# Where the bank exchange and the retention's small steps stand in the order of a two-layer decoder kernel

## The chip, the cores and the metric

The kernel runs on one core of a Trainium2 chip. Five engines work side by side and each takes its own instructions in order: TensorE (PE, matrix products), VectorE (DVE), ScalarE (ACT), GpSimd (POOL) and SyncE (SP, which issues nearly all loads). Semaphores join them. The metric is the device time of one execution in microseconds (us). A change under about 0.2% cannot be told from none here.

## The reference

Two layers over 512 tokens of width 2048, all in float32. Each layer modulates a normalised x by vectors that come from c (`shift`, `scale`, `gate`), mixes, and adds. Layer 0 mixes by retention over 8 heads, layer 1 by latent attention:

```python
for i in range(DEPTH):
    mod = (c_act @ ada_w[i] + ada_b[i])[:, None, :]
    shift, scale, gate = jnp.split(mod, 3, axis=-1)
    h = rmsnorm(x, norm_g[i]) * (1.0 + scale) + shift
    ...
    x = x + gate * y

def retention_branch(h, pos, w_in, gn_g, w_out):
    proj = h @ w_in
    q, k, v, g = jnp.split(proj, ...)
    q = rope(q, pos); k = rope(k, pos) * (RET_DK ** -0.5)
    y = chunkwise_retention(q, k, v)
    mu = jnp.mean(y, axis=-1, keepdims=True)
    var = jnp.mean(jnp.square(y - mu), axis=-1, keepdims=True)
    y = (y - mu) * lax.rsqrt(var + EPS)
    y = y.reshape(B, S, RET_WIDTH) * gn_g
    return (jax.nn.silu(g) * y) @ w_out
```

## The kernel before

**Products.** A float32 operand is split into a high part (a cast by ACT, L135 and L330) and a low part (a subtraction by DVE, L136 and L332), and a product is three matmuls: high by high, high by low, low by high. A matmul of 128x128 by 128x512 follows the one before it after 0.227 us.

**The opening** (L407 to L717) starts the projection of layer 0 while the modulation is still being summed. The 16 tiles of the 2048 columns of h ("kt") go in 8 units of two. For each unit PE does three groups of 24 matmuls, 5.44 us each: `products` of `here` and of g for both kt, and `bank_products` of `there`; `here` and `there` are v and qk by turns. v and qk need four PSUM banks each and share four, so `swap` (L385) changes them over: for each bank ACT copies its sums out (L390) and the other kind's sums in (L394), 8 copies, about 5 us. For the next unit `sum_mod` multiplies and sums two modulation loads for each kt on DVE (L356, 2.2 us each, 4 in a unit), `make_first` forms h and its high part on ACT (L370 to L381) and the low part hT on DVE (L382), and the weights of the next unit are split. `prepare_ahead(u, first, between)` and `prepare_behind` write this out; `queued` and `behind` (L422 to L433) tie what they issue behind the last instruction on ACT, DVE, PE and SP, so the code's order there is the engines' order. Unit 1 alone passes its products and its swap as `first` into `prepare_ahead`. In the last unit the tables of the rotation are made on DVE, and then the sums of h (L450 to L455), ahead of the first weights of the step list.

**The step list** follows. A step has the load and split of one tile of weights (`prepare`), its matmuls (`multiply`) and lists of small pieces `beside` it. The loop near L2180 issues, for step i: the loads, the split of the weights of step i+1 (`prepare_for`), the pieces `form` (on ACT and DVE), the matmuls, the pieces `multiply`, and then the modulation sums that have landed. A scheduler places the PE rows that `behind` does not tie, by its own estimate of when their inputs are ready.

**The retention** of a head (L1146 to L1296) is 14 pieces, one for each step, beside the out-projection of the heads ahead of it (L1390, names `o`, weights `o_r`, `o_whi`, `o_wlo`; 24 matmuls, 5.44 us in a step): rotations of q and k (`rope`, `qk_0p`), `scores` (s), their decay, `split_v` (v's parts), `values` (y), `group_norm` (statistics L1233 and L1234, the factor -mean/sd `nmr` L1239, and `yn` L1245, which reads y's banks), `gate`, `transposes` (yT), and `form_input`: the out-projection's operands `o_h` (ACT, L1275) and `o_l` (DVE, L1276). There are three rounds of 16 such steps with two heads each (heads 2 to 7), ahead of them heads 0 and 1. The even head's last pieces fall in the middle of a round; the odd head's `form_input` falls into the step that opens the next round, whose second step reads it. `light` says which steps of a round also load a row of the modulation of later stages (`mod`, L1092, a DVE sum of 1.2 us each).

Of the kernel before, what the change touches and what calls it, by code (L numbers as in the profile page):

```python
# [18 lines left out]
NT = T // P  # L19
# [30 lines left out]
def hybrid_trunk_kernel(  # L50
# [62 lines left out]
    def small(name, n=1):  # L113
        return base.tile([P, n], F32, tag="small", bufs=24, name=name)
# [316 lines left out]
    def queued(fn, *args):  # L431
        with behind(A_, V_, T_, S_):
            return fn(*args)  # L433
# [227 lines left out]
    for u in range(1, NU):  # L661

        here, there = ("v", "qk") if u % 2 == 0 else ("qk", "v")
        more = u + 1 < NU
        turns0 = [(kind, kt) for kind in (here, "g") for kt in (2 * u, 2 * u + 1)]
        if u == 1:
            def go_on_first():
                for turn in turns0:
                    queued(products, *turn)
                queued(swap, here, there)  # L670

            load_unit(2)
            prepare_ahead(2, low, go_on_first)
        elif more:
            load_unit(u + 1)
            prepare_ahead(u + 1, low)
        else:
            for i in range(7):
                if i == 2:
                    queued(low)  # L680
                queued(next, tables)
        if u == NU - 2:
            next(tables)
        if u > 1:
            for turn in turns0:
                queued(products, *turn)
        if more:
            if u > 1:
                queued(swap, here, there)
            low = prepare_behind(u + 1)  # L690
        else:
            for b, ps in enumerate(banks["qk"]):
                st = tmp(f"qk0_st{b}")
                queued(ACT.copy, st, ps)
                POOL.dma_start(qk_d[b * P : (b + 1) * P, :], st)
            queued(swap, None, "v")
            for _ in tables:
                pass
            for n, t in enumerate(ret_tables):
                POOL.dma_start(tables_d[n * P : (n + 1) * P, :], t)  # L700
            sum_parts = [queued(form_sums, n, hT, sums1, staged0, None, True) for n in range(2)]
            for b, ps in enumerate(banks["g"]):
                st = tmp(f"g0_st{b}")
                queued(ACT.activation, st, ps, AF.Silu)
                POOL.dma_start(g_d[b * P : (b + 1) * P, :], st)
        queued(bank_products, there, u)
# [24 lines left out]
    class Step:  # L731
# [3 lines left out]
        def __init__(self, load=None, prepare=None, multiply=None, follow=None, rows=0, sums=None):  # L735
            self.units = [(load, prepare)] if load else []
            self.multiply, self.follow = multiply, follow or (lambda: None)
            self.rows, self.sums = rows, sums
            self.beside = {"load": [], "form": [], "multiply": []}

    def plain_steps(nu, kn, parts, cn, name, take, n, lhs, rhs, evac, seeded=False, **kw):

# [418 lines left out]
    def retention(h, own, own2=None):  # L1161
# [64 lines left out]
                    mm3(ps, (s_hl[m][0][:, o : o + P], s_hl[m][1][:, o : o + P]), act_row(v[m]), m == 0, m == i)  # L1226
                ys.append(ps)

        def group_norm():
            stats = small(f"bn_{h}", 2 * NT)  # L1230
            for i in range(NT):
                st = l1_tile("st6", 4, f"st_{h}_{i}", (P, 6))
                DVE.bn_stats(out=st, in_=ys[i])  # L1233
                DVE.bn_aggr(out=stats[:, 2 * i : 2 * i + 2], in_=st)  # L1234
            var = small(f"var_{h}", NT)
            DVE.tensor_copy(var, stats.rearrange("p (i s) -> p i s", s=2)[:, :, 1])
            r = rsqrt(var, NT, 1.0, f"gn_{h}")
            nmr = small(f"nmr_{h}", NT)
            DVE.scalar_tensor_tensor(  # L1239
                out=nmr, in0=stats.rearrange("p (i s) -> p i s", s=2)[:, :, 0], scalar=-1.0, in1=r,  # L1240
                op0=ALU.mult, op1=ALU.mult,
            )
            for i in range(NT):
                y = l1_tile("yn", 4, f"yn_{h}_{i}")
                ACT.activation(y, ys[i], AF.Identity, bias=nmr[:, i : i + 1], scale=r[:, i : i + 1])  # L1245
                yn.append(y)
# [14 lines left out]
        def form_input():  # L1261
# [25 lines left out]
            {"load": load_decay, "multiply": scores},  # L1287
            {},
            {"load": load_v, "form": decay_scores},
            {"load": load_gates, "form": split_v, "multiply": values},  # L1290
            {"form": group_norm},
            {"form": gate},
            {"multiply": transposes},
            {"form": form_input},
        ]

    def place(pieces, block, first):
# [134 lines left out]
    for n in range(3):  # L1432
        block = []
        cols = range(4) if n % 2 == 0 else range(3, -1, -1)
        for r, after in zip(cols, [*cols[1:], None]):
            block += round_steps(n, r, go_on(n, r, after))
        heads += [retention(2 * n + 2 + i, big) for i in range(2)]
        light(block, (0, 2, 3, 4, 6, 7, 10, 11, 12, 14, 15, 0, 3, 7, 11, 15))
        steps += block


# [718 lines left out]
    for i, step in enumerate(steps):  # L2160
# [8 lines left out]
        with behind(S_):  # L2169
# [7 lines left out]
                    nc.sync.dma_start(tables[n], tables_d[(n0 + n) * P : (n0 + n + 1) * P, :])  # L2177
            for load in step.beside["load"]:
                load()
        n_prepared += prepare_for(i + 1)  # L2180
        with behind(V_, A_):
            for form_ in step.beside["form"]:
                form_()
        with behind(T_):
            step.multiply()
# [290 lines left out]
```

## Time and profile before

| | |
|---|---|
| median of 3 runs | 2158.71 us (2158.55 to 2159.61) |
| the profiled execution | 2156.47 us, its span 2154.7 us, granted clock 0.999 |
| opening, unit 1 to unit 7 | 51.83 to 163.4 us |
| step list: heads 0 and 1 and what leads to them | to about 1030 us |
| the three rounds | about 1030 to 1370 us |
| layer 1 | the rest |

In the profile's rows a start time comes first, then the duration, the engine, the line of the kernel, the operation, what it writes and reads without buffer numbers, and in brackets how long the engine had been idle before it and whose end ended that. A matmul's duration of 0.39 overlaps the next one. A window's row has the busy time of each engine, then the granted clock of PE, the share of the DMA engines and GB/s.

### The profile page before, as it was taken

To read this page: it belongs to the slowest core of one execution; us is meant where nothing else is said; L and a number is where in the kernel's file an instruction comes from. 1 tells how busy PE (TensorE), PEld (TensorE's weight loads), DVE (VectorE), ACT (ScalarE), POOL (GpSimd) and SP (SyncE) were. 2 spreads that over 40 slices of the span, in tenths; PEclk is the share of its full clock that TensorE was granted. 3 is DMA by queue.
4 is the path that set the end of the run, shared out by engine and by line. 5 is a ranking of instruction groups with operands and counts; after the bars stand their busy time and mean duration, and the time that the engine had idled before them with its cause. 6 is when DMAs were issued, how large, how long until landed. Compare 5 with 4: busy or idle time off the path is not lost.

```text
span 2154.7 us, 30027 instructions
## 1 busy us (share of the span) xinstructions
PE 2130.0 (99%) x11100; PEld 1825.1 (85%) x11100; DVE 1675.9 (78%) x2481; ACT 1056.5 (49%) x1604; POOL 106.8 (5%) x178
## 2 busy tenths in 40 slices
PE   8999999999999999999999999999999999999998
PEld 5788898988889888888888888898889989888887
DVE  7998788888878789766777787667978788886745
ACT  5674444445444444434344445345446565664434
POOL 1010000000000000000000000010001000000000
PEclk9999999999999999999999999999999999999999
DMA  9975686877777768765746566553456544346733
GB/s 382 404 277 193 220 275 225 277 236 259 257 257 256 230 234 281 247 204 167 241 159 232 188 219 244 167 174 112 165 181 208 181 135 147 116 135 222 242 108 137
DMA packets 229782, 462.96 MB, mean 215 GB/s; under 512 B 20817, under 2 KB 84337, under 8 KB 225793
## 3 DMA queue, kind: packets, MB, share of 16 engines
q1 hardware_dynamic: 217424, 421.85, 58.7%
q0 software_dynamic: 11920, 38.91, 4.6%
q8 instruction: 87, 1.43, 0.3%
q14 instruction: 61, 0.50, 0.1%
q10 hardware_dynamic: 290, 0.27, 0.0%
HBM read 417.96 MB, written 43.00 MB: 214 GB/s over the span
## 4 chain that ended last, share of the span: by engine, by line
PE 83%; DVE 6%; DMA 5%; issue 2%; ACT 2%; POOL 1%; SPq 0%; DVEq 0%; POOLq 0%; ACTq 0%
PE o L1390 9%; PE o L2312 4%; PE y L810 2%; PE y L811 2%; PE s L810 2%; PE y L809 2%; PE s L811 2%; PE x L811 2%; PE x L810 2%; PE s L809 2%; PE x L809 2%; PE x_qk L908 2%; PE y_qk L908 2%; PE s_qk L908 2%; PE qk L161 2%
## 5 line engine op out<-in xcount | busy, mean ns | idle before, releaser
L1390 PE MATMUL o<-o_h,o_whi 128*128 128x512 f32 (+1 forms) x496 | 192.2, 388 | 0.0
L1390 PE MATMUL o<-o_h,o_wlo 128*128 128x512 f32 (+1 forms) x496 | 191.4, 386 | 0.0
L1390 PE MATMUL o<-o_l,o_whi 128*128 128x512 f32 (+1 forms) x496 | 191.3, 386 | 0.0
L136 DVE TENSOR_TENSOR o_wlo<-o_r,o_whi 128x1024 fp32r<-128x1024 f32 x61 | 74.5, 1223 | 46.1 <-ACT o_whi L135 45.6
L1390 PEld LDWEIGHTS o<-o_h,o_wlo 128*128 128x128 f32 x496 | 93.2, 188 | 18.8
L1390 PEld LDWEIGHTS o<-o_h,o_whi 128*128 128x128 f32 x496 | 93.2, 188 | 18.4
L1390 PEld LDWEIGHTS o<-o_l,o_whi 128*128 128x128 f32 x496 | 93.2, 188 | 18.2
L356 DVE SCALAR_TENSOR_TENSOR aw<-aw,c_all 128x2048 f32<-128x2048 f32 (+1 forms) x35 | 73.1, 2102 | 2.4 <-DMA aw<-in_ada_t_dram 2.4
L161 PE MATMUL qk<-hT,qk_h 128*128 128x512 f32 x192 | 74.9, 390 | 0.0
L162 PE MATMUL qk<-hT,qk_h 128*128 128x512 f32 x192 | 74.7, 389 | 0.0
L135 ACT CAST o_whi<-o_r 128x1024 fp32r<-128x1024 f32 x61 | 63.5, 1051 | 21.7 <-PE o L1390 17.7
L163 PE MATMUL qk<-hT,qk_l 128*128 128x512 f32 x192 | 73.4, 389 | 0.0
L1092 DVE SCALAR_TENSOR_TENSOR mod<-mod,c_odd 128x1024 f32<-128x1024 f32 x48 | 58.0, 1219 | 18.2 <-DMA mod<-in_ada_t_dram 18.2
L136 DVE TENSOR_TENSOR o_w_lo<-o_w_raw,o_w_hi 128x1024 fp32r<-128x1024 f32 x32 | 39.0, 1220 | 33.0 <-ACT o_w_hi L135 33.0
L1092 DVE SCALAR_TENSOR_TENSOR mod<-mod,c_bm 128x1024 f32<-128x1024 f32 x48 | 58.5, 1218 | 0.0
L2312 PE MATMUL o<-o_h,o_w_hi 128*128 128x512 f32 (+1 forms) x160 | 55.6, 348 | 0.0
L2312 PE MATMUL o<-o_h,o_w_lo 128*128 128x512 f32 (+1 forms) x160 | 55.5, 347 | 0.0
L2312 PE MATMUL o<-o_l,o_w_hi 128*128 128x512 f32 (+1 forms) x160 | 55.5, 347 | 0.0
L1245 ACT ACTIVATE yn<-y,nmr,gn_r 128x512 f32<-128x512 f32 x32 | 22.3, 776 | 62.0 <-DVE nmr L1239 62.0
L135 ACT CAST o_w_hi<-o_w_raw 128x1024 fp32r<-128x1024 f32 x32 | 33.5, 1050 | 36.7 <-PE o L2312 32.7
L162 PE MATMUL o<-o_l,o_w_hi 128*128 128x512 f32 x128 | 50.1, 391 | 0.3 <-DVE o_l L136 0.3
L135 ACT CAST o_h<-o_in 128x1024 fp32r<-128x1024 f32 x24 | 25.2, 1051 | 50.9 <-PE o L162 46.9
(1607 smaller groups left out, 6899.5 us busy)
## 6 DMA issues: line engine op xcount, KB each, us to landing
mod<-in_ada_t_dram SPq DMA_DIRECT2D x96, 512.0 KB, 5.7
o_r<-in_ret_w_out_dram SPq DMA_DIRECT2D x64, 512.0 KB, 5.4
aw<-in_ada_t_dram SPq DMA_DIRECT2D x30, 1024.0 KB, 9.3
mod_gate<-in_ada_t_dram SPq DMA_DIRECT2D x32, 512.0 KB, 4.8
o_w_raw<-in_mla_w_out_dram SPq DMA_DIRECT2D x32, 512.0 KB, 4.2
qk_r<-in_ret_w_in_dram SPq DMA_DIRECT2D x48, 256.0 KB, 3.1
qk_r<-qk_d SPq DMA_DIRECT2D x32, 256.0 KB, 5.7
v_r<-v_d SPq DMA_DIRECT2D x32, 256.0 KB, 6.6
```

The costliest lines, as they stand in the source:

```text
L135: ACT.copy(hi, src)
L136: DVE.tensor_sub(lo, src, hi.bitcast(F32))
L161: PE.matmul(o, lhs[0], rhs[0], start=first and not seeded, stop=False, skip_group_check=seeded)
L162: PE.matmul(o, lhs[0], rhs[1], start=False, stop=False, skip_group_check=seeded)
L163: return PE.matmul(o, lhs[1], rhs[0], start=False, stop=last, skip_group_check=seeded)
L809: PE.matmul(banks[b], a[0], w[0], start=first, stop=False, skip_group_check=True)
L810: PE.matmul(banks[b], a[0], w[1], start=False, stop=False, skip_group_check=True)
L811: PE.matmul(banks[b], a[1], w[0], start=False, stop=True, skip_group_check=True)
L908: PE.matmul(o, w[wp][:, i, b * P : (b + 1) * P], a[ap], start=first and i + b + k == 0, stop=k == 2, skip_group_check=True,)
L1092: DVE.scalar_tensor_tensor(out=aw, in0=aw, scalar=1.0, in1=silu_c[j], op0=ALU.mult, op1=ALU.mult, accum_out=mc[:, j, b : b + 1],)
L1390: PE.matmul(o, w[i][:, ki, c0 + b * P : c0 + (b + 1) * P], a[j], start=first and i + j == 0, stop=last and i == 1, skip_group_check=True,)
L2312: PE.matmul(banks2[b][:, cols], w[0][i][:, 0, b * P : (b + 1) * P], o2_moving(w, u, cols)[j], start=u + i + j == 0, stop=u == KD - 1 and i ...
```

## The change

1. Opening: from unit 1 on, every unit that has a successor passes its products and its swap as `between` into `prepare_ahead`, so that the 8 copies stand on ACT ahead of the `make_first` of the next kt, of the cast of g's and of `there`'s weights. Before, unit 1 alone did so (by `first`). In the last unit the low part of the last kt comes one table step earlier.
2. Retention: two new places in a step. `ahead` is issued ahead of the split of the next step's weights; `split_v` and the statistics (now `norm_stats`, with the reciprocal root) are there. `late` is issued behind all pieces `form` of the step; `form_input` is there.
3. `light`: the second row of step 7 of a round moves to step 9.

On ACT, around the swap of unit 2 (`part` and `qk` are the copies out and in, `h_6f` and `hT` belong to kt 6 of unit 3), before:

```order
L370 ACTIVATE b_col_89<-mc_0_594,vcol 128x1
L372 ACTIVATE a_col_87<-mc_1_599,bias_142,vcol 128x1
L379 ACTIVATE hT_603<-xT_153,b_col_89,a_col_87 128x512
L381 ACTIVATE h_6f<-xT_153,b_col_89,a_col_87 128x512
L330 CAST g_3_k4b_610<-g_3_raw 128x1024
L330 CAST v_3_whi_613<-v_3_raw 128x1024
L390 COPY part_v_0_667<-v_7_0_518 128x512
L394 COPY qk_12_0_675<-part_qk_0_510 128x512
```

and with the change:

```order
L390 COPY part_v_0_649<-v_7_0_518 128x512
L394 COPY qk_10_0_657<-part_qk_0_510 128x512
L390 COPY part_v_1_651<-v_7_1_519 128x512
L394 COPY qk_10_1_658<-part_qk_1_512 128x512
L390 COPY part_v_2_653<-v_7_2_520 128x512
L394 COPY qk_10_2_659<-part_qk_2_514 128x512
L390 COPY part_v_3_655<-v_7_3_521 128x512
L394 COPY qk_10_3_660<-part_qk_3_516 128x512
L370 ACTIVATE b_col_89<-mc_0_594,vcol 128x1
L372 ACTIVATE a_col_87<-mc_1_599,bias_142,vcol 128x1
L379 ACTIVATE hT_667<-xT_153,b_col_89,a_col_87 128x512
L381 ACTIVATE h_6f<-xT_153,b_col_89,a_col_87 128x512
```

The first copy stood behind kt 6's h and the two casts; now the eight copies stand ahead of these.

On PE, the last matmul of the opening and the first step of the list (qk columns, `qk_0` to `qk_2` are token tiles, `qk_h` and `qk_l` the weights' parts), before:

```order
L407 MATMUL v_24_3_1353<-v_7_whi_1169,hT_1243 128x512
L161 MATMUL qk_0_1467<-hT_282,qk_0_h 128x512
L162 MATMUL qk_0_1467<-hT_282,qk_0_h 128x512
L161 MATMUL qk_1_1468<-hT_282,qk_0_h 128x512
L162 MATMUL qk_1_1468<-hT_282,qk_0_h 128x512
L161 MATMUL qk_2_1469<-hT_282,qk_0_h 128x512
L162 MATMUL qk_2_1469<-hT_282,qk_0_h 128x512
L163 MATMUL qk_0_1467<-hT_282,qk_0_l 128x512
L161 MATMUL qk_0_1467<-hT_336,qk_0_h 128x512
```

and with the change:

```order
L407 MATMUL v_24_3_1353<-v_7_whi_1233,hT_1243 128x512
L161 MATMUL qk_0_1467<-hT_282,qk_0_h 128x512
L162 MATMUL qk_0_1467<-hT_282,qk_0_h 128x512
L163 MATMUL qk_0_1467<-hT_282,qk_0_l 128x512
L161 MATMUL qk_0_1467<-hT_336,qk_0_h 128x512
L162 MATMUL qk_0_1467<-hT_336,qk_0_h 128x512
L163 MATMUL qk_0_1467<-hT_336,qk_0_l 128x512
L161 MATMUL qk_1_1468<-hT_282,qk_0_h 128x512
L162 MATMUL qk_1_1468<-hT_282,qk_0_h 128x512
```

The first matmul that reads `qk_l` was the seventh of the step and is now the third.

On DVE, in the step that opens the second round (`o1_l3` is head 3's operand, `rope_4` and `qk_4` belong to head 4, `o1_1_3_2` are the out-projection's weights), before:

```order
L136 TENSOR_TENSOR o1_1_3_2_wlo1_10149<-o1_1_3_2_r_10046,o1_1_3_2_whi0_10148 128x1024
L1156 TENSOR_TENSOR rope_4_0_0_t0_10165<-qk00_4_r_10092,cos_0_8151 128x512
L1276 SCALAR_TENSOR_TENSOR o1_l3_0_10153<-yT_3_0_10124,vcol_85,o1_h3_0_10152 128x512
L1276 SCALAR_TENSOR_TENSOR o1_l3_0_10153<-yT_3_1_10129,vcol_85,o1_h3_0_10152 128x512
L1276 SCALAR_TENSOR_TENSOR o1_l3_2_10159<-yT_3_2_10134,vcol_85,o1_h3_2_10158 128x512
L1276 SCALAR_TENSOR_TENSOR o1_l3_2_10159<-yT_3_3_10139,vcol_85,o1_h3_2_10158 128x512
L1157 TENSOR_TENSOR rope_4_0_0_t1_10166<-qk01_4_r_10094,sin_0_8153 128x512
L1158 TENSOR_TENSOR rope_4_0_0_t0_10165<-rope_4_0_0_t0_10165,rope_4_0_0_t1_10166 128x512
L136 TENSOR_TENSOR qk_4_0_0p_10164<-rope_4_0_0_t0_10165,qk_4_0_0p_10164 128x512
```

and with the change:

```order
L136 TENSOR_TENSOR o1_1_3_2_wlo1_10149<-o1_1_3_2_r_10046,o1_1_3_2_whi0_10148 128x1024
L1151 TENSOR_TENSOR rope_4_0_0_t0_10153<-qk00_4_r_10092,cos_0_8151 128x512
L1152 TENSOR_TENSOR rope_4_0_0_t1_10154<-qk01_4_r_10094,sin_0_8153 128x512
L1153 TENSOR_TENSOR rope_4_0_0_t0_10153<-rope_4_0_0_t0_10153,rope_4_0_0_t1_10154 128x512
L136 TENSOR_TENSOR qk_4_0_0p_10152<-rope_4_0_0_t0_10153,qk_4_0_0p_10152 128x512
L1274 SCALAR_TENSOR_TENSOR o1_l3_0_10161<-yT_3_0_10124,vcol_85,o1_h3_0_10160 128x512
L1274 SCALAR_TENSOR_TENSOR o1_l3_0_10161<-yT_3_1_10129,vcol_85,o1_h3_0_10160 128x512
L1274 SCALAR_TENSOR_TENSOR o1_l3_2_10167<-yT_3_2_10134,vcol_85,o1_h3_2_10166 128x512
L1274 SCALAR_TENSOR_TENSOR o1_l3_2_10167<-yT_3_3_10139,vcol_85,o1_h3_2_10166 128x512
```

The four `o1_l3` stood between the first and the second row of head 4's rotation; now they stand behind the whole of it. On ACT the four `o_h` and the cast of `qk_4_0_0p` change places in the same way.

```diff
@@ -663,32 +663,27 @@
         here, there = ("v", "qk") if u % 2 == 0 else ("qk", "v")
         more = u + 1 < NU
         turns0 = [(kind, kt) for kind in (here, "g") for kt in (2 * u, 2 * u + 1)]
-        if u == 1:
-            def go_on_first():
-                for turn in turns0:
-                    queued(products, *turn)
+
+        def turn_over():
+            for turn in turns0:
+                queued(products, *turn)
+            if more:
                 queued(swap, here, there)
 
-            load_unit(2)
-            prepare_ahead(2, low, go_on_first)
-        elif more:
+        if more:
             load_unit(u + 1)
-            prepare_ahead(u + 1, low)
+            prepare_ahead(u + 1, low, turn_over)
         else:
             for i in range(7):
-                if i == 2:
+                if i == 1:
                     queued(low)
                 queued(next, tables)
         if u == NU - 2:
             next(tables)
-        if u > 1:
-            for turn in turns0:
-                queued(products, *turn)
         if more:
-            if u > 1:
-                queued(swap, here, there)
             low = prepare_behind(u + 1)
         else:
+            turn_over()
             for b, ps in enumerate(banks["qk"]):
                 st = tmp(f"qk0_st{b}")
                 queued(ACT.copy, st, ps)
@@ -736,7 +731,7 @@
             self.units = [(load, prepare)] if load else []
             self.multiply, self.follow = multiply, follow or (lambda: None)
             self.rows, self.sums = rows, sums
-            self.beside = {"load": [], "form": [], "multiply": []}
+            self.beside = {"load": [], "ahead": [], "form": [], "late": [], "multiply": []}
 
     def plain_steps(nu, kn, parts, cn, name, take, n, lhs, rhs, evac, seeded=False, **kw):
 
@@ -1226,15 +1221,18 @@
                     mm3(ps, (s_hl[m][0][:, o : o + P], s_hl[m][1][:, o : o + P]), act_row(v[m]), m == 0, m == i)
                 ys.append(ps)
 
-        def group_norm():
-            stats = small(f"bn_{h}", 2 * NT)
+        def norm_stats():
+            stats = aside["bn"] = small(f"bn_{h}", 2 * NT)
             for i in range(NT):
                 st = l1_tile("st6", 4, f"st_{h}_{i}", (P, 6))
                 DVE.bn_stats(out=st, in_=ys[i])
                 DVE.bn_aggr(out=stats[:, 2 * i : 2 * i + 2], in_=st)
             var = small(f"var_{h}", NT)
             DVE.tensor_copy(var, stats.rearrange("p (i s) -> p i s", s=2)[:, :, 1])
-            r = rsqrt(var, NT, 1.0, f"gn_{h}")
+            aside["r"] = rsqrt(var, NT, 1.0, f"gn_{h}")
+
+        def group_norm():
+            stats, r = aside["bn"], aside["r"]
             nmr = small(f"nmr_{h}", NT)
             DVE.scalar_tensor_tensor(
                 out=nmr, in0=stats.rearrange("p (i s) -> p i s", s=2)[:, :, 0], scalar=-1.0, in1=r,
@@ -1287,11 +1285,11 @@
             {"load": load_decay, "multiply": scores},
             {},
             {"load": load_v, "form": decay_scores},
-            {"load": load_gates, "form": split_v, "multiply": values},
-            {"form": group_norm},
+            {"load": load_gates, "ahead": split_v, "multiply": values},
+            {"ahead": norm_stats, "form": group_norm},
             {"form": gate},
             {"multiply": transposes},
-            {"form": form_input},
+            {"late": form_input},
         ]
 
     def place(pieces, block, first):
@@ -1435,7 +1433,7 @@
         for r, after in zip(cols, [*cols[1:], None]):
             block += round_steps(n, r, go_on(n, r, after))
         heads += [retention(2 * n + 2 + i, big) for i in range(2)]
-        light(block, (0, 2, 3, 4, 6, 7, 10, 11, 12, 14, 15, 0, 3, 7, 11, 15))
+        light(block, (0, 2, 3, 4, 6, 7, 9, 10, 11, 12, 14, 15, 0, 3, 11, 15))
         steps += block
 
 
@@ -2177,9 +2175,12 @@
                     nc.sync.dma_start(tables[n], tables_d[(n0 + n) * P : (n0 + n + 1) * P, :])
             for load in step.beside["load"]:
                 load()
+        with behind(V_, A_):
+            for form_ in step.beside["ahead"]:
+                form_()
         n_prepared += prepare_for(i + 1)
         with behind(V_, A_):
-            for form_ in step.beside["form"]:
+            for form_ in step.beside["form"] + step.beside["late"]:
                 form_()
         with behind(T_):
             step.multiply()
```

## The prediction

> **What bounds the kernel now.** I read the engines' busy shares first, then the list of PE's waits, then the timeline at each wait.
>
> ```profile
> PE 2130.0 (99%) x11100; PEld 1825.1 (85%) x11100; DVE 1675.9 (78%) x2481; ACT 1056.5 (49%) x1604; POOL 106.8 (5%) x178
> ```
>
> TensorE is busy for 2130.0 of 2154.7 us, and the change takes no matmul away. It can only save stops of PE. The list of waits says how much that is at the places that are touched (columns: total us, times, longest):
>
> ```profile
> PE qk L407 <- ACT qk L394: 2.4, 1, 2.4
> ...
> PE s L161 <- ACT yn L1245: 1.0, 4, 0.3
> ...
> PE y L162 <- DVE v L136: 0.2, 1, 0.2
> ```
>
> The first is the bank exchange of unit 2 in the opening; the other two are the heads' scores waiting for the group norm to read the banks of y, and y waiting for the low part of v. So some 3.6 us, plus what each stop costs beside its wait, is the whole prize; the rest of the working asks how much of it becomes time, and what is late next.
>
> **Opening.** Starts of PE's products g of units 1, 2 and 7, the stop, and the first matmul after the opening:
>
> ```profile
> 51.83 5.61 PE L407 MATMUL g<-hT,g_k4b 128*128 128x512 f32 x24
> ...
> 68.16 5.60 PE L407 MATMUL g<-hT,g_k4b 128*128 128x512 f32 x24
> 76.20 0.50 PE L407 MATMUL qk<-hT,qk_whi 128*128 128x512 f32 x1 [2.44 <-ACT qk L394]
> ...
> 152.54 5.60 PE L407 MATMUL g<-hT,g_k4b 128*128 128x512 f32 x24
> ...
> 163.42 0.39 PE L161 MATMUL qk<-hT,qk_h 128*128 128x512 f32 x1
> ```
>
> Unit 1, which has the new order already, lasts 68.16 - 51.83 = 16.33 us. Five units at that pace are 81.6 us; they take 152.54 - 68.16 = 84.38. The difference, 2.78 us, is lost in unit 2 (a 2.44 us wait and a slow restart); in the later units the old order loses nothing. So this part can gain 2.78 us at most, once.
>
> Does the new order hold 16.33 us in every unit? Unit 1 shows it, with the row that DVE comes to behind "there"'s low part:
>
> ```profile
> 57.54 0.80 ACT L381 ACTIVATE h_4f<-xT,b_col,a_col 128x512 f32<-128x512 f32 x1
> ...
> 58.37 0.69 DVE L382 TENSOR_TENSOR hT<-h_4f,hT 128x512 fp32r<-128x512 f32 x1 [1.72 <-ACT h_4f L381]
> ...
> 63.81 2.28 DVE L356 SCALAR_TENSOR_TENSOR aw<-aw,c_all 128x2048 f32<-128x2048 f32 x1
> ...
> 142.95 0.42 DVE L255 CAST ret_sin<-ret_pi 128x512 f32<-128x512 int32 x1
> ...
> 159.11 0.43 DVE L455 TENSOR_TENSOR sums_f<-h_f,sums_f 128x256 f32<-128x256 f32 x1
> 160.53 1.22 DVE L136 TENSOR_TENSOR qk_l<-qk_r,qk_h 128x1024 fp32r<-128x1024 f32 x1 [0.99 <-ACT qk_h L135]
> ...
> 165.49 1.23 DVE L136 TENSOR_TENSOR qk_l<-qk_r,qk_h 128x1024 fp32r<-128x1024 f32 x1 [1.34 <-ACT qk_h L135]
> ```
>
> The eight copies, which stand ahead of h, make DVE wait 1.72 us for h_4f, but PE runs through. What follows that wait is tied to PE, so DVE comes to the same point of each unit 63.81 - 51.83 = 11.98 us after PE's g. That is the price. With the new order g of unit 6 starts at 68.16 + 4 x 16.32 = 133.44, so DVE reaches the tables of the rotation (142.95 before) at 133.44 + 11.98 = 145.42, 2.47 us later than now, although PE is 2.78 us earlier. From there to 159.54 DVE works without a pause (tables, then sums of h), so the next work, qk_l of the first step, moves from 159.54 to about 162.0 and ends at 163.2; its present 0.99 us wait for ACT is used up. PE arrives at that step at 163.42 - 2.78 = 160.64, and in the order of the changed kernel qk_l is needed by the third matmul instead of the seventh: 160.64 + 2 x 0.227 = 161.09. It stops for 163.2 - 161.1 = 2.1 us, and 0.1 for the restart. Net: -2.78 + 2.2 = **-0.6 us**. Bounds: -2.8, if DVE's work there is not in the way, and +0.5, if a second step is late too (the next qk_l has 1.34 us of wait to use up, so I take none). Loads and the queue of SP are in the same order here; the copies only change places on ACT, whose waits they share. The load buffers come free up to 2.5 us later on DVE, and so do their readers: nothing.
>
> On the stop itself the row says that 2.44 us of idle PE cost nothing afterwards:
>
> ```profile
> 68.00:84.00 16.00, 13.56 (x60) 10.89 (x59) 14.81 (x15) 11.67 (x19) 0.00 (x0) 1.00 1.02 409
> ```
>
> the granted clock (third number from the end) is 1.00 through that stretch. [...]
>
> **Retention: what is gained.** PE at head 0, at the second pair's head 2, and at head 4 (s are scores, y is values):
>
> ```profile
> 979.36 0.50 PE L161 MATMUL s<-qk_0p,qk_0p 128*128 128x512 f32 x1 [0.30 <-ACT yn L1245]
> 979.70 0.39 PE L162 MATMUL s<-qk_0p,qk_0p 128*128 128x512 f32 x1
> ...
> 1091.14 0.39 PE L1390 MATMUL o<-o_h,o_wlo 128*128 128x512 f32 x1
> 1091.78 0.50 PE L161 MATMUL s<-qk_0p,qk_0p 128*128 128x512 f32 x1 [0.25 <-ACT yn L1245]
> ...
> 1191.28 0.39 PE L1390 MATMUL o<-o_h,o_wlo 128*128 128x512 f32 x1
> 1191.58 1.19 PE L161 MATMUL y<-v,sT 128*128 128x512 f32 x4
> 1192.92 0.50 PE L162 MATMUL y<-v,sT 128*128 128x512 f32 x1 [0.15 <-DVE v L136]
> ...
> 1304.59 1.19 PE L161 MATMUL y<-v,sT 128*128 128x512 f32 x4
> ```
>
> A restart takes 979.70 - 979.36 = 0.34 us to the next matmul where 0.227 is usual, 0.11 more. Head 0: 0.30 + 0.11 = 0.4. Head 2: 1091.78 - 1091.14 - 0.227 + 0.11 = 0.5. Head 4: from 1191.28 to 1192.92 are 1.64 us for five matmuls, 1.13 usual, so 0.5 and 0.11: 0.6; head 6, 113.01 us later, alike: 0.6. All four go if v's parts and the statistics come ahead of the next o_w low part, which stands in their way:
>
> ```profile
> 1191.04 1.23 DVE L136 TENSOR_TENSOR o_wlo<-o_r,o_whi 128x1024 fp32r<-128x1024 f32 x1 [0.26 <-ACT o_whi L135]
> 1192.18 2.49 DVE L136 TENSOR_TENSOR v<-v_r,v 128x512 fp32r<-128x512 f32 x4
> ```
>
> DVE's 1.14 us for o_wlo are then behind v (its reader on PE is a step of 5.44 us away), and v is in time. Sum **-2.1 us**. The two other s waits (heads 4 and 6, 0.5 each) stay, since PE comes to them 0.6 us earlier as well. Bounds: -3.1 with these, -0.5 if only head 2's holds.
>
> **Retention: what is late next.** The pieces put last ("late") are moved behind the other work of the step. In the step that opens the next round the rotation of the next head (cos, sin, sum, qk's low part) now stands ahead of the odd head's four o_h on ACT and four o_l on DVE, and PE's next step begins with these. Before, DVE, ACT and PE:
>
> ```profile
> 1139.35 1.23 DVE L1092 SCALAR_TENSOR_TENSOR mod<-mod,c_odd 128x1024 f32<-128x1024 f32 x1 [2.45 <-DMA mod<-in_ada_t_dram]
> ...
> 1141.64 0.69 DVE L1156 TENSOR_TENSOR rope_t<-qk_r,cos 128x512 f32<-128x512 f32 x1
> 1142.24 2.72 DVE L1276 SCALAR_TENSOR_TENSOR o_l<-yT,vcol,o_h 128x512 fp32r<-128x512 f32 x4
> 1144.88 0.68 DVE L1157 TENSOR_TENSOR rope_t<-qk_r,sin 128x512 f32<-128x512 f32 x1
> 1145.59 0.69 DVE L1158 TENSOR_TENSOR rope_t<-rope_t,rope_t 128x512 f32<-128x512 f32 x1
> 1146.97 0.69 DVE L136 TENSOR_TENSOR qk_0p<-rope_t,qk_0p 128x512 fp32r<-128x512 f32 x1 [0.69 <-ACT qk_0p L135]
> ...
> 1137.59 2.42 ACT L1275 ACTIVATE o_h<-yT,vcol 128x512 fp32r<-128x512 f32 x4 [5.01 <-PE yT L1258]
> ...
> 1144.17 0.39 PE L1390 MATMUL o<-o_h,o_whi 128*128 128x512 f32 x1
> 1144.40 0.39 PE L1390 MATMUL o<-o_l,o_whi 128*128 128x512 f32 x1
> ...
> 1254.08 0.69 DVE L1156 TENSOR_TENSOR rope_t<-qk_r,cos 128x512 f32<-128x512 f32 x1 [0.25 <-DMA qk_r<-qk_d]
> ```
>
> Counted in the order of PE, the matmuls at 1144.17 and 1144.40 are the first that read head 3's o_h and o_l. Now DVE would do cos at 1141.64, sin at 1142.24, the sum 0.71 later at 1142.95, and qk's low part 1.38 after that (as 1145.59 to 1146.97, ACT's cast between them) at 1144.33. o_h starts on ACT behind that cast, near 1144.25, and its first is there at 1144.85 (2.42 / 4); the first o_l starts on DVE 0.6 behind qk's low part, 1144.93, and is there at 1145.6 (2.72 / 4). PE wants it at 1144.40: a stop of 1.2 us, 1.3 with the restart. For head 5 PE is 113.01 us later, the cos of DVE only 1254.08 - 1141.64 = 112.44: 0.6 less, 0.7 us. Head 1 has no such stop (its step leaves DVE some 2 us), head 7 no rotation behind it. The odd heads' y, whose banks come free later with o_l, I put at 0.1 us each. Sum **+2.2 us**. Bounds: 0, if DVE's work ahead (which waits 2.45 us for a modulation load) comes as early as PE does; +4.0, if PE is early by the 0.9 us of heads 0 and 2 and DVE is not, at both places.
>
> The third part, a modulation row two steps later, moves one 1.2 us sum on DVE and its 512 KB load; it lies beside PE work in a stretch where DVE has waits, and I cost it at nothing, with 0.3 either way.
>
> **Sum.** -0.6 - 2.1 + 2.2 = -0.5 us. The profiled execution took 2156.47 us, so 2156.0 after; its median of runs is 2158.71, 2.24 more, and from that: **2158.2 us**.
>
> **The rivals.**
> 1. The waits vanish and nothing takes their place: -2.8 - 2.6 (heads 0, 2, 4, 6 and one of the two s waits) = -5.4, 2153.3 us, -0.25%. For it: DVE is busy 78% only. Against it: at 142.95 to 159.54 DVE has no pause at all.
> 2. Slower: the stop before head 3's and head 5's o_l follows the modulation load. Each us by which that load lands later goes to PE twice, since it stands ahead of the rotation which is now ahead of o_l. At 2.5 us later (as much as it is waited for now) it is +5.0: 2163.2 us. It decides from 2.4 us on (2 x 2.4 - 0.5 = 4.3). Speaks for it: SP's loads are in another order there, v's ahead of the modulation's. Against it: those loads are steps away from this place. [...]
> 3. The opening does not gain and the retention's "late" piece costs in full: +0.5 - 0.5 + 4.0 = +4.0, 2162.7 us.
> 4. The change does what it says in the opening only up to the tables, and the retention's gain and loss are both half of mine: -0.6, which no run would tell from my forecast.
>
> **Chances and range.** A measurement of this kernel tells about 0.2%, 4.3 us, from no change: 2154.4 to 2163.0. My forecast with rival 4: 0.65. Rival 1: 0.16, of which 0.12 end under 2154.4. Rival 3: 0.08, of which 0.03 over 2163.0. Rival 2: 0.11, nearly all over it. So faster 0.12, same 0.74, slower 0.14. The forecast's own bounds are -2.8 - 3.1 + 0 and +0.5 - 0.5 + 4.0, 2152.8 to 2162.7; both ends together are unlikely, and 8 in 10 lie between 2154.0 and 2162.5.
>
> **What would show it.** Opening: no wait of PE at L407 near 73 us, g of unit 7 near 149.8; then a wait of PE at the first qk step near 161 us for DVE's qk_l, of about 2 us. If that wait is missing, the opening gained all of 2.8. Retention: the waits of y for v and of s near 979 and 1091 gone; new waits of o at the line of the out-projection for o_l, about 1.3 and 0.7 us, once at the beginning of the second and once of the third round. Wrong it would be if units 3 to 6 last over 16.4 us, if those new waits are over 3 us, or if PE waits for loads.

## The result, and the profile after

The changed kernel takes 2166.11 us (median of 7 runs, 2161.67 to 2168.69), the kernel before 2158.55 us in the same series (7 runs, 2157.55 to 2159.80): 1.0032 times the time before, 95% interval 1.0021 to 1.0042. The forecast was 2158.2 us, with 8 chances in 10 for a time between 2154.0 and 2162.5. The profiled execution of the changed kernel took 2165.86 us, 9.4 more than that of before, with the span 2164.1 us; by the medians the difference is 7.6 us. Lines of code after the opening are numbered a little lower: L1390 is L1388 now, L1275 and L1276 (o_h, o_l) are L1273 and L1274, L1245 (yn) is L1243.

The list of PE's waits (total us, times, longest):

```profile
PE o L1388 <- ACT o_h L1273: 4.2, 2, 2.2
...
PE s L161 <- ACT yn L1243: 2.8, 3, 1.1
...
PE qk L163 <- DVE qk_l L136: 1.5, 1, 1.5
...
PE o L1388 <- DVE o_l L1274: 0.6, 2, 0.3
```

The wait for the bank exchange (2.4 us) and that of y for v (0.2) are gone. New are a wait for qk_l and two for o_h, and the scores wait longer for yn (2.8 us for 1.0).

The opening in the timeline: g of unit 7, the end of unit 6 on DVE, and PE and DVE at the first step of the list:

```profile
149.87 0.62 PE L407 MATMUL g<-hT,g_k4b 128*128 128x512 f32 x2
...
145.54 0.42 DVE L255 CAST ret_sin<-ret_pi 128x512 f32<-128x512 int32 x1
...
160.90 0.50 PE L161 MATMUL qk<-hT,qk_h 128*128 128x512 f32 x1
...
163.18 0.50 PE L163 MATMUL qk<-hT,qk_l 128*128 128x512 f32 x1 [1.55 <-DVE qk_l L136]
...
161.91 1.22 DVE L136 TENSOR_TENSOR qk_l<-qk_r,qk_h 128x1024 fp32r<-128x1024 f32 x1
```

PE is 2.67 us earlier at unit 7 (149.87 for 152.54), and DVE 2.59 us later at the tables (145.54 for 142.95).

The beginning of the second round, on PE and DVE, and the stop at that of the third:

```profile
1142.96 0.39 PE L1388 MATMUL o<-o_h,o_wlo 128*128 128x512 f32 x1
1145.32 0.50 PE L1388 MATMUL o<-o_h,o_whi 128*128 128x512 f32 x1 [1.98 <-ACT o_h L1273]
1146.12 0.80 PE L1388 MATMUL o<-o_l,o_whi 128*128 128x512 f32 x1 [0.30 <-DVE o_l L1274]
1146.72 0.63 PE L1388 MATMUL o<-o_h,o_wlo 128*128 128x512 f32 x1
1147.14 0.63 PE L1388 MATMUL o<-o_h,o_whi 128*128 128x512 f32 x1
...
1260.73 0.39 PE L1388 MATMUL o<-o_h,o_wlo 128*128 128x512 f32 x1
1263.36 0.50 PE L1388 MATMUL o<-o_h,o_whi 128*128 128x512 f32 x1 [2.24 <-ACT o_h L1273]
...
1141.93 0.69 DVE L1151 TENSOR_TENSOR rope_t<-qk_r,cos 128x512 f32<-128x512 f32 x1
...
1145.32 2.72 DVE L1274 SCALAR_TENSOR_TENSOR o_l<-yT,vcol,o_h 128x512 fp32r<-128x512 f32 x4
```

After the stop the matmuls follow one another by 0.42 to 0.43 us (1147.14 after 1146.72) where 0.227 is usual. The windows show why; the third number from the end is the granted clock, before and behind each stop:

```profile
1143.00:1146.50 3.50, 1.23 (x4) 0.57 (x3) 2.78 (x5) 2.44 (x5) 0.00 (x0) 0.92 0.92 321
1146.50:1150.00 3.50, 3.50 (x11) 2.69 (x10) 3.50 (x6) 1.44 (x2) 0.00 (x0) 0.60 0.51 203
1261.00:1264.00 3.00, 0.62 (x2) 0.19 (x1) 2.28 (x4) 1.90 (x4) 0.00 (x0) 1.00 0.96 343
1264.00:1268.50 4.50, 4.34 (x13) 3.42 (x14) 4.46 (x8) 1.98 (x3) 0.00 (x0) 0.65 0.44 172
```

And the scores of head 4, with the group norm on DVE and POOL:

```profile
1208.39 0.50 PE L161 MATMUL s<-qk_0p,qk_0p 128*128 128x512 f32 x1 [1.13 <-ACT yn L1243]
...
1205.16 0.17 DVE L129 TENSOR_SCALAR gn_v<-var 128x4 f32<-128x4 f32 x1
1205.24 1.23 DVE L136 TENSOR_TENSOR o_wlo<-o_r,o_whi 128x1024 fp32r<-128x1024 f32 x1
1207.37 0.16 DVE L1237 SCALAR_TENSOR_TENSOR nmr<-bn,gn_r 128x4 f32<-128x4 f32 x1 [0.90 <-POOL gn_r L131]
...
1205.41 1.92 POOL L131 TENSOR_TENSOR gn_r<-gn_v,mhalf 128x4 f32<-128x4 f32 x1 [82.24 <-DVE gn_v L129]
```

How late PE is against the kernel before, at matmuls that are the same in both timelines (start after less start before):

| place | us later | what happened since the last row |
|---|---|---|
| g of unit 7 | -2.67 | the exchange's stop gone |
| behind head 0 (994.68 for 995.90) | -1.22 | qk_l's stop +2.1, head 0's scores -0.6 |
| head 3's yT (1137.63 for 1138.62) | -0.99 | head 2's scores wait 0.25 longer |
| head 4's scores (1208.39 for 1204.78) | +3.61 | stop and slow clock +4.3, y -0.6, scores +0.9 |
| ahead of head 5's o_h (1255.42 for 1251.63) | +3.79 | 0.1 to 0.2 at y of head 5 |
| head 6's scores (1326.54 for 1317.79) | +8.75 | stop and slow clock +4.7, y -0.6, scores +0.9 |
| end of the span (2164.1 for 2154.7) | +9.4 | small differences behind that, most of them in layer 1 |

Of the 4.3 and 4.7 us, the stops are 2.8 and 3.1 (from 1142.96 to the second restart, and alike at 1260.73), the slow clock behind them 1.5 and 1.6.

### The profile page after: what moved, and what is told of

Read it like the earlier page. It is cut to its first block, busy times and chain, and to the rows that moved or that the text cites. A ratio compares the mean times of both kernels' runs of the same rounds, so it can differ in the third digit from the quotient of the medians.

```text
span 2164.1 us, 30043 instructions
## 1 busy us (share of the span) xinstructions
PE 2134.5 (99%) x11100; PEld 1827.9 (84%) x11100; DVE 1676.4 (77%) x2481; ACT 1057.2 (49%) x1604; POOL 114.1 (5%) x178
## 4 chain that ended last, share of the span: by engine, by line
PE 86%; DVE 5%; DMA 4%; issue 2%; ACT 2%; POOL 1%; SPq 0%; POOLq 0%; DVEq 0%; ACTq 0%
PE o L1388 12%; PE o L2313 4%; PE y L805 2%; PE y L806 2%; PE s L805 2%; PE y L804 2%; PE s L806 2%; PE x L806 2%; PE x L805 2%; PE s L804 2%; PE x L804 2%; PE x_qk L903 2%; PE y_qk L903 2%; PE s_qk L903 2%; PE qk L163 2%; PE qk L161 2%
## 5 line engine op out<-in xcount | busy, mean ns | idle before, releaser
L1388 PE MATMUL o<-o_h,o_whi 128*128 128x512 f32 (+1 forms) x496 | 193.7, 390 | 4.2 <-ACT o_h L1273 4.2
L1388 PE MATMUL o<-o_l,o_whi 128*128 128x512 f32 (+1 forms) x496 | 192.9, 389 | 0.6 <-DVE o_l L1274 0.6
L1388 PE MATMUL o<-o_h,o_wlo 128*128 128x512 f32 (+1 forms) x496 | 192.5, 388 | 0.0
L1388 PEld LDWEIGHTS o<-o_h,o_whi 128*128 128x128 f32 x496 | 93.8, 189 | 23.6 <-ACT o_h L1273 5.1
L1388 PEld LDWEIGHTS o<-o_l,o_whi 128*128 128x128 f32 x496 | 94.0, 190 | 19.8 <-DVE o_l L1274 1.2
L1388 PEld LDWEIGHTS o<-o_h,o_wlo 128*128 128x128 f32 x496 | 94.0, 190 | 18.9
L1243 ACT ACTIVATE yn<-y,nmr,gn_r 128x512 f32<-128x512 f32 x32 | 22.3, 778 | 66.0 <-DVE nmr L1237 66.0
```

The lines of the kernel that those rows point to most:

```text
L1388: PE.matmul(o, w[i][:, ki, c0 + b * P : c0 + (b + 1) * P], a[j], start=first and i + j == 0, stop=last and i == 1, skip_group_check=True,)
```

## The experiments

Each ran beside the kernel before on the same chip; ratios are against these runs, 2157.9 to 2158.3 us.

**form_input back in its place.** In the changed kernel:

```diff
-            {"late": form_input},
+            {"form": form_input},
```

> The changed kernel with form_input back among the pieces 'form' and all else as changed. My theory: the late form_input makes PE stop for head 3's and head 5's o_h (2.0 and 2.2 us in the changed kernel), and each stop is followed by about ten matmuls at a lower granted clock (2.2 us each). Without it there are no waits of o for o_h, the granted clock is 1.00 through the beginnings of the second and third round, and some 9 us go: about 2157.5 us, runs within 1 us of each other like those of before. What stays: the scores' waits for yn (1.1 us for heads 4 and 6). Rival 1, the loads in their new order make o_h late: then the waits stay and the time is about 2166. Rival 2, the clock dips by itself: then the runs still scatter over some 5 us and single runs show a clock of 0.997.

2158.63 us (2157.44 to 2160.70, 11 runs), ratio 1.0004 (0.9995 to 1.0013). The waits for o_h are gone, and every run's mean clock is 0.998 or 0.999 (0.995 to 0.999 in the changed kernel). So the late form_input is what costs some 7 us in the changed kernel (each taken against the runs beside it, 7.6 and 0.4 us over the kernel before). The order of the loads isn't the cause, since it is still the changed one. The profiled execution's mean clock is 0.999, for 0.997 in the changed kernel. The time is 1.1 us over my expectation: o_wlo and o_h now make a few small stops of 0.1 to 0.5 us in the next round. The runs lie 3.3 us apart, where I expected about 1.

**The opening alone** (the first hunk of the diff on the kernel before).

> Only the opening's part of the change. My theory: -2.8 us from unit 2's stop, +2.1 from the new stop for the first step's qk_l, so 0.6 to 0.7 us faster than before: about 2157.9. Rival: the opening gains all 2.8 us (2155.8) or, with the stop followed by a lower clock, loses (over 2159).

2156.69 us (2155.46 to 2158.40, 11 runs), ratio 0.9993 (0.9985 to 1.0002); its profiled execution is 0.4 us faster than that of before. The stop for qk_l is there with 1.5 us of wait. The median is 1.5 us under the runs beside it, where 0.6 to 0.7 was expected; the sign is as expected, but the interval takes in no change.

**The late piece alone** (on the kernel before, only form_input behind the pieces `form`):

```diff
-            for form_ in step.beside["form"]:
+            for form_ in step.beside["form"] + step.beside["late"]:
...
-            {"form": form_input},
+            {"late": form_input},
```

> The kernel before with form_input behind the other pieces 'form', and nothing else. PE comes to the two places about 1 us later than in the changed kernel, since nothing was gained ahead. My theory: stops for o_h of about 1.2 us at head 3 and 1.3 at head 5, so +2.5 us if such stops leave the clock alone: 2161.0; +6.5 if also these are followed by a lower clock: 2165. Rival: the late piece costs nothing without the other parts: 2158.5.

2161.51 us (2159.33 to 2164.35, 11 runs), ratio 1.0019 (1.0010 to 1.0028). PE at the two places:

```profile
1147.71 0.49 PE L1390 MATMUL o<-o_h,o_whi 128*128 128x512 f32 x1 [0.87 <-ACT o_h L1275]
1148.51 0.50 PE L1390 MATMUL o<-o_l,o_whi 128*128 128x512 f32 x1 [0.31 <-DVE o_l L1276]
1148.85 0.40 PE L1390 MATMUL o<-o_h,o_wlo 128*128 128x512 f32 x1
...
1263.04 0.50 PE L1390 MATMUL o<-o_h,o_whi 128*128 128x512 f32 x1 [1.27 <-ACT o_h L1275]
```

The stops are 1.7 and 2.1 us with the second wait, for o_l, and the restarts, and the pitch behind them is the usual one (1148.85 after 1148.51 is a restart, then 0.23). The two come to 3.8 us, the median is 3.3 us over the runs beside it, and the clock costs nothing at these places. But in this same execution the clock fell in the opening, behind the exchange's stop of unit 2, which had left it alone in the kernel before. Windows in and behind that stop, here and then in the kernel before:

```profile
75.00:78.00 3.00, 0.88 (x4) 0.75 (x5) 2.95 (x2) 2.90 (x6) 0.00 (x0) 1.00 1.02 427
78.00:82.00 4.00, 4.00 (x12) 3.16 (x11) 3.84 (x5) 3.84 (x8) 0.00 (x0) 0.57 1.03 409
```

```profile
75.00:78.00 3.00, 1.80 (x8) 1.48 (x9) 3.00 (x4) 2.87 (x6) 0.00 (x0) 1.00 1.00 418
78.00:82.00 4.00, 4.00 (x19) 3.32 (x18) 2.94 (x4) 3.81 (x8) 0.00 (x0) 1.00 1.04 410
```

The same wait of 2.4 us costs some 1.5 us more in one execution (12 matmuls in 4 us for 19) than in the other: the clock is 0.57 behind it here and 1.00 in the kernel before.

**Statistics, nmr and yn in one piece.** On the first of these kernels, all of the group norm ahead of the next weights:

```diff
-            {"ahead": norm_stats, "form": group_norm},
+            {"ahead": lambda: (norm_stats(), group_norm())},
```

> The first of these kernels, and in it also nmr and yn directly behind the statistics, so that no weights' low part of DVE stands beside the reciprocal root on POOL. My theory: gn_r on POOL takes 1.0 us again (1.9 in the changed kernel, where DVE's o_wlo runs at the same time), nmr comes 0.9 us earlier, and the waits of the scores fall from 0.7, 1.1 and 1.1 us to at most 0.4 each: 2 to 2.5 us less than the first of these kernels, about 2155.3. Rival: POOL's time has another reason, gn_r stays at 1.9 and the gain is under 0.5 us; or yn ahead of the next cast on ACT makes o_whi late, with a new wait of PE for the out-projection's weights.

2166.19 us (2165.09 to 2168.85, 5 runs), ratio 1.0042 (1.0028 to 1.0056), 10.9 us over my expectation. The reciprocal root on POOL, all eight heads, in the changed kernel and then here (min/median/max ns):

```profile
L131 POOL TENSOR_TENSOR gn_r<-gn_v,mhalf x8: 1893/1922/1942, 974.9 to 1357.2; 128x4 f32<-128x4 f32 x8
```

```profile
L131 POOL TENSOR_TENSOR gn_r<-gn_v,mhalf x8: 1007/1009/1040, 975.4 to 1355.6; 128x4 f32<-128x4 f32 x8
```

So gn_r takes 1.0 us where DVE's o_wlo doesn't run beside it, and the scores wait 0.4 us in all. The rival's other half came true as well, and was larger: ACT does yn ahead of the next cast, and PE waits for its result.

```profile
PE o L1388 <- ACT o_whi L135: 3.1, 3, 1.0
PE y L161 <- DVE o_l L1274: 2.5, 3, 1.3
```

**The retention's parts alone** (all hunks of the diff but the first; the opening as before).

> The retention's parts of the change (ahead, late, light) with the opening as before. My theory: the stops for head 3's and head 5's o_h are there with some 2 us each, and in most executions the granted clock falls behind one or both of them, 2.2 us each time: 2162 to 2167 by execution, median about 2165.5; opening alone (0.7 us faster in trace) and this then add up to the whole change. Rival: the large loss needs both parts, since the opening brings PE ahead of DVE: then this kernel is near the late piece alone, 2161 to 2162.

2166.17 us (2163.77 to 2169.20, 6 runs), ratio 1.0036 (1.0024 to 1.0048): all of the loss. In the profiled execution the stops before o_h last 1.5 and 2.2 us, for 2.1 and 2.4 in the changed kernel. So the opening's gain doesn't add: PE that comes earlier waits longer for o_h. The mean clock of this execution is 0.998, as with the late piece alone, for 0.997 with the two falls of the changed kernel. That fits one fall, by an estimate from the 3.41 us at 0.50 of each fall there, which take 0.0008 off the mean; after the first 24 us PE has two waits of over 2 us here, 2.1 before o_h and 2.4 at the exchange of unit 2.

**Two table steps into units 5 and 6.** On the opening alone:

```diff
         queued(sum_mod, 2 * u + 1, 0)
+        if u >= NU - 2:
+            queued(next, tables)
         queued(low)
...
-            for i in range(7):
+            for i in range(5):
...
-        if u == NU - 2:
+        if u == NU - 4:
             next(tables)
```

> The opening's part alone, and two of the rotation tables' seven queued steps (7 instructions of DVE, about 3.2 us) moved ahead into units 5 and 6, to the place where DVE waits for h. My theory: DVE's table work behind unit 6 is what makes qk_l of the first step late; with 3.2 us less of it the stop of 1.5 us (with its restart 1.8) goes, and nothing new comes, since the new place lies in a wait of DVE of 1 to 1.7 us: 1.8 us less than the opening alone, 2154.9, 0.13 to 0.15% under the kernel before. Rival: DVE has no such room there, h and hT come later, and units 6 and 7 last over 16.4 us: the time stays at 2156.5 or more.

2154.99 us (2153.46 to 2156.17, 11 runs), ratio 0.9983 (0.9974 to 0.9992). DVE comes to qk_l 3.2 us earlier than in the changed kernel, and PE runs into the first step without a stop:

```profile
158.67 1.22 DVE L136 TENSOR_TENSOR qk_l<-qk_r,qk_h 128x1024 fp32r<-128x1024 f32 x1
```

**The same, and split_v ahead** (statistics, form_input and light as before).

> The kernel with the tables spread, and of the retention's parts only split_v ahead of the next weights (statistics, late and light as before). My theory: y of heads 4 and 6 finds its v in time, 0.6 us each; POOL's gn_r takes 1.0 us; the scores' waits stay at about 0.4 us: 1.2 us less than the kernel before this one in the list, 2153.7. Rival: v ahead makes o_wlo or the odd head's o_l late and the gain is given back: 2154.9 or more.

2154.34 us (2152.92 to 2155.73, 9 runs), ratio 0.9980 (0.9970 to 0.9989). It is 0.65 us less than without split_v, half of what I expected, and the two intervals overlap, so the runs alone don't show it. In the trace y's waits are gone, but the scores of heads 4 and 6 wait 0.6 us each for yn, for 0.2 to 0.3 before: so about half of the gain is given back there.

**light as before.** On the first of these kernels, the modulation rows of the kernel before:

```diff
-        light(block, (0, 2, 3, 4, 6, 7, 9, 10, 11, 12, 14, 15, 0, 3, 11, 15))
+        light(block, (0, 2, 3, 4, 6, 7, 10, 11, 12, 14, 15, 0, 3, 7, 11, 15))
```

> The changed kernel with form_input in its old place and also the modulation rows of light as before; statistics and v ahead, opening as changed. My theory: the row that was moved to step 9 has its 1.2 us DVE sum directly ahead of the statistics and so delays them; with it gone nmr of heads 2, 4 and 6 comes about 1.1 us earlier, and the scores' waits of 0.7, 1.1 and 1.1 us nearly vanish even though gn_r still takes 1.9 us: about 2.5 to 3 us less than with form_input alone put back, 2155.8. Rival: the moved row is not what delays nmr: 2158.5 as there.

2155.20 us (2153.49 to 2158.86, 11 runs), ratio 0.9984 (0.9975 to 0.9993): 3.4 us less than with the moved row. DVE ahead of head 4's statistics, in the changed kernel and then here:

```profile
1200.33 0.69 DVE L136 TENSOR_TENSOR qk_1p<-rope_t,qk_1p 128x512 fp32r<-128x512 f32 x1 [0.69 <-ACT qk_1p L135]
1200.94 1.22 DVE L1087 SCALAR_TENSOR_TENSOR mod<-mod,c_odd 128x1024 f32<-128x1024 f32 x1
```

```profile
1196.45 0.69 DVE L136 TENSOR_TENSOR qk_1p<-rope_t,qk_1p 128x512 fp32r<-128x512 f32 x1 [0.69 <-ACT qk_1p L135]
1197.06 1.29 DVE L1228 BATCH_NORM_STATS2 st<-y 128x6 f32<-128x512 f32 x2
```

The statistics start right behind qk_1p, without the row's sum of 1.15 us between, and the list has no wait of the scores for yn, although gn_r still takes 1.92 us here. So the third part of the change, which I had costed at nothing, costs 3.4 us. It does so beside the slower gn_r: with the row moved but gn_r at 1.01 us, in the kernel with nmr and yn in one piece, the scores wait only 0.4 us in all.

**The stop filled.** The whole change, and ten matmuls more ahead of the first ones that read the late o_h:

```diff
+                if u == 2 and (n, r) in ((1, 3), (2, 0)):
+                    for _ in range(10):
+                        PE.matmul(
+                            o1_banks[n, r, 0], w[0][:, 0, :P], o1_in[n, 0][0][:, 0, :], start=False, stop=False,
+                            skip_group_check=True,
+                        )
                 for ki, t in order:
```

> The whole change, and PE gets ten matmuls more (2.27 us) ahead of the first that read head 3's and head 5's o_h, so that it works through most of each stop instead of standing still. They add one product of the out-projection ten times over into a bank, so part of the out-projection's sum is not the reference's; the order of all else is the changed kernel's. My theory: the stops themselves cost 4.5 us in the changed kernel and PE's lower clock behind them 4.4 us. The ten matmuls take the place of the stop, so its time stays, while the clock has no idle stretch to fall after: no matmul at a pitch of 0.43 us behind these places, and 2161.5 us, with runs about 2 us apart as with the kernels without such stops. Rival: the clock falls there for another reason, such as work in the rotation's stretch: then it falls here too and the time stays near 2166, with runs 5 us apart.

2162.73 us (2160.58 to 2164.44, 11 runs), ratio 1.0022 (1.0013 to 1.0031): 3.4 us less than the changed kernel, or 2.8 with each taken against the runs beside it, with 4.5 us more of PE work. The two intervals overlap; the clock is the plainer evidence. The windows that showed 0.92, 0.60, 1.00 and 0.65 show 1.00:

```profile
1143.00:1146.50 3.50, 3.50 (x16) 2.74 (x15) 2.81 (x5) 2.84 (x6) 0.00 (x0) 1.00 0.92 299
1146.50:1150.00 3.50, 3.50 (x17) 2.88 (x16) 3.49 (x5) 1.03 (x2) 0.00 (x0) 1.00 0.48 191
...
1264.00:1268.50 4.50, 4.50 (x21) 3.74 (x20) 3.78 (x6) 1.57 (x2) 0.00 (x0) 1.00 0.01 4
```

All 11 runs have a mean clock of 0.998 or 0.999, and they lie 3.9 us apart (2 expected, 7 in the changed kernel). So the low clock at these places follows from PE standing still, and it is worth some 3 us of the loss; the stops are the rest. My price for it, 4.4 us, was too high by what the profiled execution shows (3.1).

**The parts that pay, together:** opening as changed with the two table steps moved, statistics and v ahead, form_input and light as before.

> Opening as changed with two table steps moved into units 5 and 6, statistics and v ahead as changed, form_input and the modulation rows of light as before. My theory: the gains of its parts add up, 1.8 us from the opening's second stop on the kernel with light as before (2155.2): 2153.4 us, 0.22% under the kernel before. Rival: PE, 1.8 us earlier, comes to another late work in the step list, and the time stays over 2154.3.

2153.23 us (2151.71 to 2156.47, 11 runs), ratio 0.9978 (0.9969 to 0.9987). It is below both kernels, by 0.22% (the runs beside it) and 0.59% (the changed kernel's median). None of the waits that the change is about is left in its list.

## Why the prediction was wrong, point by point

- **Opening.** Right in mechanism and size. DVE at the tables: 145.42 forecast, 145.54 measured. qk_l: 162.0 and 161.91. PE's stop with its restart: 2.2 forecast, 2.1 measured (four matmuls from 160.52 to 163.51 take 2.99 us, 0.91 is usual). Net -0.6, and -2.67 + 2.1 = -0.6 in the traces. That DVE's tables are the cause is shown by the spread steps, with which this stop is gone and the median 1.7 us lower than with the opening alone.
- **What is gained in the retention.** y of heads 4 and 6 came as priced, 0.6 us each. Head 0's scores, priced at 0.4, brought 0.6: I had counted the idle time and the restart, not the whole distance from the matmul before (978.67 to 979.36). Head 2's scores, priced at 0.5 us of gain, lost 0.25, and those of heads 4 and 6, which I let stay at 0.5 each, cost 1.4 each with the restart. Two steps failed. "The third part ... I cost it at nothing": the moved row's sum stands directly ahead of the statistics; with the row in its old place 3.4 us are saved. And "DVE's 1.14 us for o_wlo" I took to be free wherever it stands; between gn_v and nmr it makes POOL's gn_r take 1.92 us for 1.01. Where only one of the two was there, the scores waited 0.4 us in all or not at all; together they cost the 2.0 us.
- **What is late next.** The mechanism is the one forecast, at both places and on the two tiles named (most of the wait is for o_h, where I had named o_l), but the term, +2.2 us, was mis-sized. Alone it measures 3.8 us, stops of 1.7 and 2.1 us, in the profiled execution (3.3 us by the medians); head 5's was not shorter, as I took from DVE's 0.6 us of lead, but longer. In the whole change the stops are 2.8 and 3.1. At head 3 DVE's sum of the modulation row, which waits for its load and stands ahead of the rotation, starts where it did (1139.45 for 1139.35), while PE comes 1.0 us earlier. I had that as an upper bound (+4.0), not as the likeliest value, though my own sum had just made PE earlier. At head 5 that sum itself is late, before and then in the changed kernel:

```profile
1251.47 1.22 DVE L1092 SCALAR_TENSOR_TENSOR mod<-mod,c_odd 128x1024 f32<-128x1024 f32 x1 [1.56 <-DMA mod<-in_ada_t_dram]
```

```profile
1257.19 1.23 DVE L1087 SCALAR_TENSOR_TENSOR mod<-mod,c_odd 128x1024 f32<-128x1024 f32 x1 [2.12 <-DMA mod<-in_ada_t_dram]
```

It is 5.7 us later, PE only 3.8 (1260.73 for 1256.96), so DVE has lost some 1.9 us to PE there. With the late piece alone it has lost 1.6 (1257.45, and PE at 1261.38).
- **The clock.** That "2.44 us of idle PE cost nothing afterwards" was read from one execution, and is wrong for this kernel: with the late piece alone the same stop was followed by a clock of 0.57 (78 to 82 us), and in the changed kernel's profiled execution the clock fell behind both stops before o_h (windows at 0.60 and 0.65). I put the clock at nothing in the sum; it costs some 3 us. That stops of about 2 us would not lower it was my assumption, and that one execution was all that spoke for it: in the changed kernel the waits are 1.98 and 2.24 us.
- **The rivals.** The second, slower, is nearest (head 3's and head 5's operands late at the two rounds' beginnings). Its cause, a modulation load that lands later, holds at head 5 alone; at head 3 the load is not later, PE is earlier. The fall of the clock behind these stops, 3.1 us of the profiled execution, comes on top. The first, that all waits vanish, is what the best kernel shows, once form_input and light are left alone and DVE's tables spread.
- **The sum.** -0.6 - 2.1 + 2.2 stands against, in the profiled execution, -0.6 (opening), -0.6 (head 0), -1.2 (y), +2.0 (scores), +5.9 (stops), +3.1 (clock) and some +0.8 of small differences: +9.4. That is one execution; by the medians it is +7.6.

## What to carry to other kernels

Where work is moved ahead, ask for each instruction what it is now ahead of, and look there for the row with the least slack; here the piece that was put last was the one that PE needed next, and a modulation row that was moved as if it could stand anywhere came to stand on the chain that PE waits for. Price a new stop of PE together with what the earlier terms of the same sum do to it: PE that gains a microsecond waits a microsecond longer at the next late operand (head 3's o_h: PE 1.0 us earlier, a wait of 1.98 us for 0.87 with the late piece alone). A stop of two microseconds was more than its own length here: look at the granted clock behind it, in more than one execution; the exchange's stop of 2.4 us was free in one and cost 1.5 us more in another.

## What the runs showed of the hardware

- In the changed kernel the granted clock fell to 0.50 behind both stops before o_h (waits of 1.98 and 2.24 us), for 3.41 us each time, from 1145.91 and from 1265.38; six and seven matmuls then came 0.43 us apart, and 1.5 and 1.6 us were lost. With the late piece alone it fell behind the exchange's stop of unit 2 (2.4 us). The mean clock of the profiled executions is 0.997 in the changed kernel, 0.998 with the late piece alone, with the retention's parts alone and with light as before (where one wait after the first 24 us is over 2 us, 2.1 of v for hT), and 0.999 in the other eight. Two of these eight have such a wait too: the kernel before (2.4, the exchange of unit 2, clock 1.00 behind it) and the statistics in one piece (2.2, v for hT). So stops of this length were followed by a fall in some executions and not in others. Shorter ones had none behind them: 1.55 us for qk_l in the changed kernel, whose two falls are those named, and 1.6 at g with the opening alone, whose mean is 0.999.
- Where the stop lies may have a part in that. The two low stretches of the changed kernel start 119.47 us apart, 35 times 3.4133; the clock falls once more behind the end of PE's work, 894.29 us after the second, 262 times 3.4133. Windows of that length, first the changed kernel (the stop of head 3, the low stretch, the next), then the late piece alone, the kernel before, and the statistics in one piece, each with its stop:

```profile
1142.50:1145.91 3.41, 1.35 (x5) 0.56 (x3) 2.69 (x5) 1.85 (x4) 0.00 (x0) 1.00 0.84 295
1145.91:1149.33 3.42, 3.21 (x8) 2.53 (x9) 3.42 (x6) 2.03 (x3) 0.00 (x0) 0.50 0.69 272
1149.33:1152.74 3.41, 3.41 (x16) 2.79 (x15) 2.69 (x5) 1.57 (x2) 0.00 (x0) 1.00 0.00 0
...
75.09:78.50 3.41, 1.38 (x6) 1.16 (x7) 3.41 (x4) 3.28 (x6) 0.00 (x0) 1.00 0.99 414
...
72.06:75.47 3.41, 1.71 (x8) 1.09 (x6) 3.27 (x5) 3.41 (x5) 0.00 (x0) 1.00 1.05 419
...
32.59:36.00 3.41, 1.56 (x7) 0.94 (x5) 1.57 (x3) 1.06 (x2) 0.00 (x0) 1.00 1.01 402
```

An estimate: counted back in steps of 3.4133 us from the fall behind the end of PE's work in the kernel before (2150.78), one step lies at 75.47, inside the exchange's stop (73.77 to 76.20), and PE is busy 1.71 us in the window ahead of it. The late piece alone has a window of this length with PE busy 1.38 us, and the clock is 0.57 from 78 to 82; the statistics in one piece have one with 1.56 us, at a mean of 0.999. In the changed kernel PE is busy 1.35 us in the window ahead of the first low stretch and 1.72 in that ahead of the second (1261.97 to 1265.38). That the step through the stop kept the clock up in the kernel before is not shown: no run moved a stop against the steps, and 1.72 with a fall beside 1.71 without leaves open what decides.
- Runs of the changed kernel lie 7 us apart, the fastest with a mean clock of 0.999 and the slowest with 0.995. That fits stops that bring a low stretch in some executions and not in others; the runs that were not profiled don't show where their clock fell.
- A POOL operation on four numbers for each partition (gn_r) took 1.01 us where DVE stood idle beside it (median of eight in the kernel before, and with the statistics in one piece) and 1.92 us in the changed kernel (1.89 to 1.94 in eight). At head 4 there DVE's o_wlo, a subtraction of o_whi from o_r, had started 0.17 us earlier (1205.24 and 1205.41), and gn_r ended 0.86 us behind it (1207.33 and 1206.47). How the one slows the other, no run shows.
